# Two weight blocks of 141 granules laid apart, in wider weight tiles

## The chip, the cores and the metric

The kernel runs on one core of one Trainium2 chip. Its metric is device time in microseconds of that core, the median of several runs. Float32 is used throughout; a product of two matrices is made of three matmuls on fp32r halves (high x high, high x low, low x high).

## The reference

A block of two layers (normalisation, bidirectional mLSTM, dilated attention, gated MLP) is followed by a second block of two layers on the same 256 tokens and on 256 context tokens (attention with a window and a sink, MLP; then a gated linear scan, MLP). Cut to what matters:

```
for l in range(2):                                   # first block, x: 256 x 1024
    u = h * (1 + sc1) + sh1                          # sc, sh, g from c_act @ w_ada[l]
    z = u @ w_in[l]                                  # mLSTM q, k, v, o, gates; attention; branch gates
    y = (sig(g_a) * (mlstm(z) @ w_a) + sig(g_b) * (dilated_attention(z) @ w_b)) @ w_out
    h = layer_norm(ALPHA * h + g1 * y)
    u = h * (1 + sc2) + sh2
    h = layer_norm(ALPHA * h + g2 * ((silu(u @ w1) * (u @ w3)) @ w2))     # 1024 -> 2816 -> 1024
for i in range(2):                                   # second block, tokens and context
    x = x + m[2] * rms_norm(attention(modulate(x)) if i == 0 else gated_scan(modulate(x)))
    x = x + m[5] * rms_norm(relu(modulate(x) @ w_mlp_in) ** 2 @ w_mlp_out) # 1024 -> 4096 -> 1024
```

## The kernel before

All weights stand in one tensor in the order of their use, packed on the host into granules of 128 x 1024 numbers (512 KB). `plan()` lists them with a key each: `va`, `at`, `qk`, `o`, `br`, `wb`, `wa`, `wo` for the mixers of the first block, `w1`, `w3`, `w2` for its MLPs, `qkv`, `awo`, `mi`, `mo` for the second block's attention and MLPs, `gq`, `gg`, `gk`, `gv`, `gwo` for its scan. 591 of them go through the main stream; 192 more (`w_ada`, `w_mod_2`) are read by VectorE alone.

`gran(key, mm, post)` takes the next granule and issues its matmuls. `ahead` runs before each: it loads raw tiles up to five granules ahead (SP's queue, four tiles), makes wh, the fp32r high half, three ahead (ScalarE, four tiles) and wl, the low half, two ahead (VectorE, three tiles). The order of all work is written out by hand: generators in a list (`bg`) hand out a piece of attention, convolution, scan or normalisation at each `tick`, between granules.

Two shapes of granule matter here. In a "ws" granule (`mm_ws`) eight blocks of 128 columns are loaded one after the other as the stationary operand, and 256 columns of an activation stream past each, three times: wh with the high half, wh with the low half, wl with the high half. A "row" granule (`w2`) does the same with eight outputs. So each is 24 matmuls of 256 columns. In a "nat" granule (`mm_nat`) the weights stream, 512 columns at a time, 12 matmuls.

```
    def mm3(self, out, wh, wl, act, first, last):
        mm = self.nc.tensor.matmul
        mm(out, wh, act[:, 0], start=first, stop=False)
        mm(out, wh, act[:, 1], start=False, stop=False)
        mm(out, wl, act[:, 0], start=False, stop=last)
```

The pools lie in SBUF one behind another: constants, `wp` (raw, wh, wl and three `araw`, each 4,096 bytes a partition), a gap of 448 bytes, the ring `t4` of 25 tiles of 4,096 bytes (activations as uT, hT, yat, mT, hid, attention's kT and qT, residuals), the ring `t2` of eight tiles of 2,048 bytes, and small tiles. A new t4 tile takes the place that has been free longest and waits for its last reader.

In the profile nearly all instructions of TensorE and VectorE carry line 338, the wrapper that records them, so that tiles tell them apart: "mm<-uT,wh" is a matmul of a ws granule, "aux<-mlg,wh" one of w2, "aux<-wh,hid" one of a nat granule of the MLP, "trb<-kT,qT" attention's scores. The copies to wh are line 471, made in `ahead`.

Of the kernel before, what the change touches and what calls it, by code (L numbers as in the profile page):

```python
# [9 lines left out]
F32 = mybir.dt.float32  # L10
F32R = mybir.dt.float32r
BF16 = mybir.dt.bfloat16
AF = mybir.ActivationFunctionType
ALU = mybir.AluOpType
# [145 lines left out]
         [("wb", 2), ("wb", 3)] + [("br", j) for j in range(8)])  # L160
ADA_ORDER = (1, 0, 2, 4, 3, 5)
PLAN, NMAIN = plan()
GIDX = {e[0]: i for i, e in enumerate(PLAN)}


def pack_weights(inp):
    out = np.empty((len(PLAN), 128, 1024), np.float32)
    for i, (key, w, l, kind, r0, c0) in enumerate(PLAN):
        W = inp[w][l]
        if kind == "ws":  # L170
            out[i] = W[:, c0:c0 + 128].reshape(8, 128, 128).transpose(1, 0, 2).reshape(128, 1024)
        elif kind == "nat":
            out[i] = W[r0:r0 + 256, c0:c0 + 512].reshape(2, 128, 512).transpose(1, 0, 2).reshape(128, 1024)
        elif kind == "wsb":
            out[i] = W[r0:r0 + 512, c0:c0 + 256].reshape(4, 128, 256).transpose(1, 0, 2).reshape(128, 1024)
        elif kind == "colT":
            out[i] = W[:, c0:c0 + 128].T
        elif kind == "row":
            out[i] = W[r0:r0 + 128, c0:c0 + 1024]
        elif kind == "gates":  # L180
            t = np.zeros((128, 8, 4, 32), np.float32)
            t[:, :, :, 0:4] = W[:, c0:c0 + 16].reshape(8, 128, 4, 4).transpose(1, 0, 2, 3)
            out[i] = t.reshape(128, 1024)
        elif kind == "gdown":
            t = np.zeros((128, 8, 4, 32), np.float32)
            t[:, :, 0:2, 0:16] = W.reshape(2, 8, 128, 16).transpose(2, 1, 0, 3)
            out[i] = t.reshape(128, 1024)
    return out

# [94 lines left out]
def host(inp):  # L286
    inp = {k: np.asarray(v) for k, v in inp.items()}
    r = {"w": pack_weights(inp), "vec": pack_vecs(inp), "x": np.ascontiguousarray(inp["x"][0][ORDER]),
         "abias": attention_bias(), "mmask": mlstm_masks(), "rope": rope_tables(), "bmask": block2_masks(),
         "c": np.ascontiguousarray(np.concatenate([cols(inp[k]) for k in ("c", "c_2", "c_ctx_2")], 1)),  # L290
         "ctx": np.ascontiguousarray(inp["ctx_2"][0]),
         "ln": np.ascontiguousarray(np.broadcast_to(np.stack([inp["ln2_g"][1], inp["ln2_b"][1]])[:, None], (2, 128, 1024))),
         "wup": np.ascontiguousarray(inp["gla_w_gate_up_2"][0])}
    return r
# [14 lines left out]
class Views(list):  # L309


    def __init__(self, views, pair):
        super().__init__(views)
        self.pair = pair


class Lazy:
# [5 lines left out]
    def __getitem__(self, k):  # L323
        return self.f(k)
# [52 lines left out]
class Kernel:  # L377
# [55 lines left out]
        return self.p2.tile(list(shape), dt, tag="t2", name=name, bufs=8)  # L433

    def t4(self, name, shape, dt=F32):
        return self.p4.tile(list(shape), dt, tag="t4", name=name, bufs=25)

    def tv(self, name, shape):

# [20 lines left out]
    def ahead(self, n):  # L460

        nc = self.nc
        while True:
            if self.nload < min(self.nlo + self.RAWS, n + self.LOAD + 1, NMAIN):
                t = self.wp.tile([128, 1024], F32, tag="raw", name="raw", bufs=self.RAWS)
                nc.sync.dma_start(out=t, in_=self.i["w"][self.nload])
                self.raws[self.nload] = t
                self.nload += 1
            elif self.nhi < min(self.nload, n + self.HI + 1):
                wh = self.wp.tile([128, 1024], F32R, tag="wh", name="wh", bufs=4)  # L470
                nc.scalar.activation(out=wh, in_=self.raws[self.nhi], func=AF.Copy)  # L471
                self.hi[self.nhi] = wh
                self.nhi += 1
            elif self.nlo < min(self.nhi, n + self.LO + 1):
                raw, wh = self.raws.pop(self.nlo), self.hi.pop(self.nlo)
                wl = self.wp.tile([128, 1024], F32R, tag="wl", name="wl", bufs=3)
                nc.vector.tensor_tensor(out=wl, in0=raw, in1=wh.bitcast(F32), op=ALU.subtract)
                self.W[self.nlo] = wh, wl
                self.nlo += 1
            else:  # L480
                break

    def gran(self, key, mm, post=None):

        self.run_deferred()
        w = self.G(key)
        mm(*w)
        if post is not None:
            self.later(1, post)
        self.tick()  # L490
# [57 lines left out]
    def ada_load(self, n, tile=None):  # L548
        for it in self.adaq[:n]:
            key = it[:4]  # L550
            if key not in self.adaraw:
                t = tile() if tile else self.wp.tile([128, 1024], F32, tag="araw", name="araw", bufs=3)
                self.nc.sync.dma_start(out=t, in_=self.i["w"][GIDX[key]])
                self.adaraw[key] = t

    def ada_step(self, ahead=3):
        nc = self.nc
        self.ada_load(ahead)
        w, l, v, j, cs, bias = self.adaq.pop(0)
        g = self.adaraw.pop((w, l, v, j))  # L560
        for c, dst in cs:
            junk = g if c is cs[-1][0] else self.p.tile([128, 1024], BF16, tag="junk", name="junk", bufs=1)
            nc.vector.tensor_tensor_reduce(out=junk, in0=g, in1=c, scale=1.0, scalar=0.0, op0=ALU.mult, op1=ALU.add,
                                           accum_out=dst[:, j:j + 1])
        self.ada_left[(w, l, v)] -= 1
        if self.ada_left[(w, l, v)] == 0 and bias is not None:
            for c, dst in cs:
                nc.vector.tensor_tensor(out=dst, in0=dst, in1=bias, op=ALU.add)
# [33 lines left out]
    def first_ws(self, keys, out, act, between=None):  # L602

        w, ahead = [], (self.HI, self.LO)

        def part(n, ks):
            for k in ks:
                c = slice(k * 128, k * 128 + 128)
                self.mm3(out[:, n * 256:n * 256 + 256], w[n][0][:, c], w[n][1][:, c], act(k), n == 0 and k == 0, n == 1 and k == 7)
        for n, key in enumerate(keys):  # L610
            self.HI, self.LO = (a - n for a in ahead)
            self.gran(key, lambda wh, wl: (w.append((wh, wl)), part(n, range(6))))
        if between is not None:
            between()
        part(0, (6, 7))
        self.HI, self.LO = ahead
        self.ahead(self.cur - 1)
        part(1, (6, 7))
# [22 lines left out]
    def last_nat(self, key, act, banks, done):  # L641

        w, ahead = [], (self.HI, self.LO)
        for kp in (2, 3):
            self.HI, self.LO = (a + 2 - kp for a in ahead)
            self.gran(key(kp), lambda wh, wl: (w.append((wh, wl)), self.mm_nat(kp, act, banks, (0,))(wh, wl)))
        done(0)
        for _ in range(3):
            self.tick(False)
        for kp in (2, 3):  # L650
            self.mm_nat(kp, act, banks, (1,))(*w[kp - 2])
        done(1)
        self.HI, self.LO = ahead
# [1602 lines left out]
```

## Time and profile before

| | us |
|---|---|
| median of 3 runs (lowest, highest) | 2083.51 (2081.5, 2088.59) |
| the profiled execution, its own time | 2092.44 |
| its span, first to last instruction | 2090.7 |
| TensorE busy in it | 2030.9 |
| VectorE busy | 1586.6 |
| ScalarE busy | 1149.3 |

The profile is one execution, and its time is not the median. "Busy" of TensorE counts the modelled length of each matmul, which overlaps that of the next; what a matmul costs in a stream is the distance from its start to the next one's start. In a window over the profile, x is the number of instructions that overlap it.

### The profile page before, as it was taken

To read this page: it belongs to the slowest core of one execution; us is meant where nothing else is said; L and a number is where in the kernel's file an instruction comes from. 1 tells how busy PE (TensorE), PEld (TensorE's weight loads), DVE (VectorE), ACT (ScalarE), POOL (GpSimd) and SP (SyncE) were. 2 spreads that over 40 slices of the span, in tenths; PEclk is the share of its full clock that TensorE was granted. 3 is DMA by queue.
4 is the path that set the end of the run, shared out by engine and by line. 5 is a ranking of instruction groups with operands and counts; after the bars stand their busy time and mean duration, and the time that the engine had idled before them with its cause. 6 is when DMAs were issued, how large, how long until landed. Compare 5 with 4: busy or idle time off the path is not lost.

```text
span 2090.7 us, 38245 instructions
## 1 busy us (share of the span) xinstructions
PE 2030.9 (97%) x15176; PEld 1888.9 (90%) x15176; DVE 1586.6 (76%) x2717; ACT 1149.3 (55%) x1968; POOL 45.1 (2%) x63
## 2 busy tenths in 40 slices
PE   7999999999999999998999999999999999999998
PEld 6999998899998989998999988899998989877997
DVE  7788988799978989988899776777563485466555
ACT  5756665655546656665744455556542464445444
POOL 0000000000000000000000000000000010000000
PEclk9999999999999999999999999999999999999999
DMA  9786566598876886555589755115553352214553
GB/s 340 281 320 213 192 235 221 187 315 305 304 254 228 284 274 233 187 202 186 167 290 358 274 196 176 61 56 176 191 183 101 115 181 75 77 65 155 188 191 132
DMA packets 120884, 426.88 MB, mean 204 GB/s; under 512 B 13664, under 2 KB 18528, under 8 KB 120704
## 3 DMA queue, kind: packets, MB, share of 16 engines
q1 hardware_dynamic: 120704, 424.43, 59.1%
q8 instruction: 119, 1.95, 0.4%
q14 instruction: 61, 0.50, 0.1%
HBM read 423.33 MB, written 1.05 MB: 203 GB/s over the span
## 4 chain that ended last, share of the span: by engine, by line
PE 87%; DVE 7%; ACT 4%; issue 1%; DMA 1%; POOL 0%; DVEq 0%; POOLq 0%; SPq 0%; ACTq 0%
PE mm L338 54%; PE aux L338 28%; PE trb L338 5%; DVE wl L338 1%; ACT wh L471 1%; DVE yg L338 1%; POOL rs L674 0%; ACT xh L1467 0%; DVE mtmp L338 0%; DMA raw<-in_w 0%; DVE xh L338 0%; DVE x L338 0%; DVE araw L338 0%; ACT ah L912 0%; DVE ee L338 0%
## 5 line engine op out<-in xcount | busy, mean ns | idle before, releaser
L338 DVE TENSOR_TENSOR wl<-raw,wh 128x1024 fp32r<-128x1024 f32 x591 | 718.7, 1221 | 153.1 <-PE aux L338 71.5
L471 ACT ACTIVATE wh<-raw 128x1024 fp32r<-128x1024 f32 x591 | 623.6, 1059 | 336.2 <-PE mm L338 117.7
L338 PE MATMUL mm<-uT,wh 128*128 128x256 f32 x3488 | 622.3, 282 | 0.0
L338 PEld LDWEIGHTS mm<-uT,wh 128*128 128x128 f32 x3488 | 531.7, 188 | 2.2 <-ACT va L814 0.3
L338 PE MATMUL mm<-uT,wl 128*128 128x256 f32 x1744 | 487.0, 279 | 0.0
L338 PE MATMUL mm<-hT,wh 128*128 128x256 f32 x1888 | 339.4, 283 | 4.8 <-ACT y L1772 2.1
L338 PEld LDWEIGHTS mm<-uT,wl 128*128 128x128 f32 x1744 | 329.6, 189 | 0.0
L338 PEld LDWEIGHTS mm<-hT,wh 128*128 128x128 f32 x1888 | 292.7, 190 | 11.5 <-ACT y L1772 2.3
L338 PE MATMUL mm<-hT,wl 128*128 128x256 f32 x944 | 265.8, 282 | 0.0
L338 DVE CUSTOM_DVE_ANT_0 araw<-araw,silu 128x1024 f32<-128x1024 f32 x192 | 233.2, 1220 | 8.4 <-DMA araw<-in_w 5.9
L338 PE MATMUL aux<-wh,hid 128*128 128x512 f32 x640 | 199.9, 394 | 0.0
L338 PEld LDWEIGHTS mm<-hT,wl 128*128 128x128 f32 x944 | 181.4, 192 | 0.0
L338 PEld LDWEIGHTS aux<-wh,hid 128*128 128x128 f32 x640 | 117.7, 188 | 23.6 <-DVE hid L338 0.2
L338 DVE TENSOR_TENSOR r<-r 128x256 f32<-128x256 f32 (+1 forms) x88 | 39.5, 448 | 117.4 <-ACT r L1905 117.3
L338 PE MATMUL aux<-mlg,wh 128*128 128x256 f32 x704 | 127.1, 283 | 0.0
L338 PE MATMUL aux<-wl,hid 128*128 128x512 f32 x320 | 124.8, 390 | 0.0
L338 PEld LDWEIGHTS aux<-mlg,wh 128*128 128x128 f32 x704 | 107.3, 188 | 0.0
L1905 ACT ACTIVATE r<-mm 128x256 f32<-128x256 f32 (+1 forms) x88 | 35.7, 406 | 125.1 <-PE mm L338 125.1
L338 PE MATMUL aux<-mlg,wl 128*128 128x256 f32 x352 | 98.8, 281 | 0.0
L674 POOL TENSOR_TENSOR rs<-ve,mhalf 128x1 f32<-128x1 f32 (+1 forms) x48 | 41.8, 871 | 2040.5 <-DVE ve L338 1853.0
L338 DVE CUSTOM_DVE_ANT_0 junk<-araw,silu 128x1024 bf16<-128x1024 f32 x64 | 77.9, 1218 | 0.0
L338 PE MATMUL mm<-wh,hT 128*128 128x256 f32 (+1 forms) x352 | 76.8, 316 | 0.6 <-DVE qs L338 0.6
(365 smaller groups left out, 3081.7 us busy)
## 6 DMA issues: line engine op xcount, KB each, us to landing
raw<-in_w SPq DMA_DIRECT2D x591, 512.0 KB, 3.9
araw<-in_w SPq DMA_DIRECT2D x192, 512.0 KB, 5.2
abias<-in_abias SPq DMA_DIRECT2D x32, 192.0 KB, 5.6
xc<-in_ctx SPq DMA_DIRECT2D x4, 512.0 KB, 6.1
x<-in_x SPq DMA_DIRECT2D x2, 512.0 KB, 4.2
gb<-in_ln SPq DMA_DIRECT2D x2, 512.0 KB, 5.4
out_x<-x SPq DMA_DIRECT2D x4, 256.0 KB, 2.0
mk<-in_mmask SPq DMA_DIRECT2D x1, 512.0 KB, 5.9
```

The source lines that it names most:

```text
L338: return f(*a, **k)
L471: nc.scalar.activation(out=wh, in_=self.raws[self.nhi], func=AF.Copy)
L674: nc.gpsimd.tensor_tensor(out=rs, in0=ve, in1=self.mhalf[:, 0:n], op=ALU.pow)
L1905: nc.scalar.activation(out=r[:, 0:n], in_=ps, func=AF.Relu)
```

## The change

The tensor of weights gets rows of 1,088 numbers in place of 1,024. For 141 granules of the main stream, chosen by key in `moved`, the host puts blocks 2 to 7 first, at columns 0 to 767, and blocks 0 and 1 behind them at columns 816 to 1,071; 48 columns between are zero. The tiles raw, wh and wl are 1,088 wide; load, copy and subtraction take 1,072 columns of such a granule and 1,024 of any other. `Moved` maps a block's old columns to the new ones, so that the matmuls and their order stay as they are. The ring t4 has 24 tiles in place of 25.

```
+WIDE = 1088
+def moved(key):
+    n = key[0]
+    if n in ("w3", "w2"):
+        return key[1] == 0
+    if n == "w1":
+        return key[1] == 1 and key[2] % 2 == 0
+    if n in ("o", "br", "wa", "wo"):
+        return key[2] % 2 == 0
+    if n == "qk":
+        return key[4] == 0
+    if n == "mi":
+        return key[2] % 4 == 0
+    return n in ("gq", "gg", "gk") and key[1] % 2 == 0
+
+class Moved:
+    def __init__(self, t):
+        self.t = t
+    def __getitem__(self, i):
+        rows, c = i
+        n = 816 if c.start < 256 else -256
+        return self.t[rows, c.start + n:c.stop + n]
...
+        if i < NMAIN and moved(key):
+            t = wide[i, :, 0:1024].copy()
+            wide[i] = 0
+            wide[i, :, 0:768] = t[:, 256:]
+            wide[i, :, 816:1072] = t[:, 0:256]
...
-        return self.p4.tile(list(shape), dt, tag="t4", name=name, bufs=25)
+        return self.p4.tile(list(shape), dt, tag="t4", name=name, bufs=24)
...
-                t = self.wp.tile([128, 1024], F32, tag="raw", name="raw", bufs=self.RAWS)
-                nc.sync.dma_start(out=t, in_=self.i["w"][self.nload])
+                t = self.wp.tile([128, WIDE], F32, tag="raw", name="raw", bufs=self.RAWS)
+                c = self.width(self.nload)
+                nc.sync.dma_start(out=t[:, c], in_=self.i["w"][self.nload][:, c])
...
-                nc.scalar.activation(out=wh, in_=self.raws[self.nhi], func=AF.Copy)
+                c = self.width(self.nhi)
+                nc.scalar.activation(out=wh[:, c], in_=self.raws[self.nhi][:, c], func=AF.Copy)
...
-                nc.vector.tensor_tensor(out=wl, in0=raw, in1=wh.bitcast(F32), op=ALU.subtract)
-                self.W[self.nlo] = wh, wl
+                nc.vector.tensor_tensor(out=wl[:, c], in0=raw[:, c], in1=wh.bitcast(F32)[:, c], op=ALU.subtract)
+                self.W[self.nlo] = (Moved(wh), Moved(wl)) if moved(PLAN[self.nlo][0]) else (wh, wl)
...
+    def width(self, n):
+        return slice(0, 1072 if moved(PLAN[n][0]) else 1024)
...
-                self.nc.sync.dma_start(out=t, in_=self.i["w"][GIDX[key]])
+                self.nc.sync.dma_start(out=t, in_=self.i["w"][GIDX[key]][:, 0:1024])
```

## Rows read from the trace of the kernel before

**Rows 1.** The page, parts 1 and 4: busy time, and the chain by engine.
```profile
PE 2030.9 (97%) x15176; PEld 1888.9 (90%) x15176; DVE 1586.6 (76%) x2717; ACT 1149.3 (55%) x1968; POOL 45.1 (2%) x63
...
PE 87%; DVE 7%; ACT 4%; issue 1%; DMA 1%; POOL 0%; DVEq 0%; POOLq 0%; SPq 0%; ACTq 0%
```
**Rows 2.** Windows, TensorE: length, busy (x matmuls), granted clock, DMA share, GB/s.
```profile
606.00:626.00 20.00, 20.00 (x179) 1.00 0.55 185
...
1042.00:1218.00 176.00, 176.00 (x1496) 1.00 0.82 295
...
1498.00:1518.00 20.00, 20.00 (x172) 1.00 0.54 178
...
1609.00:1652.00 43.00, 43.00 (x368) 1.00 0.27 91
285.00:294.00 9.00, 9.00 (x79) 1.00 0.54 173
```
**Rows 3.** Timeline, TensorE, at 608 us: start, length, line, operation, count.
```profile
607.84 0.39 PE L338 MATMUL aux<-mlg,wh 128*128 128x256 f32 x2
...
608.52 0.39 PE L338 MATMUL aux<-mlg,wh 128*128 128x256 f32 x2
```
**Rows 4.** Timeline, TensorE, at 1100 us.
```profile
1099.89 0.40 PE L338 MATMUL mm<-uT,wh 128*128 128x256 f32 x2
...
1100.60 0.40 PE L338 MATMUL mm<-uT,wh 128*128 128x256 f32 x2
```
**Rows 5.** Timeline, TensorE, at 575 us: w1, scores, w3.
```profile
574.44 0.39 PE L338 MATMUL mm<-uT,wh 128*128 128x256 f32 x2
...
575.12 0.64 PE L338 MATMUL trb<-kT,qT 128*128 128x256 f32 x4
575.60 0.40 PE L338 MATMUL mm<-uT,wh 128*128 128x256 f32 x2
...
576.30 0.28 PE L338 MATMUL mm<-uT,wh 128*128 128x256 f32 x1
```
**Rows 6.** Timeline, TensorE, at 421 us: transposes, scores, w3.
```profile
420.81 0.49 PE L338 MATMUL trb<-ident,qs 128*128 128x128 f32 x3
421.06 0.73 PE L338 MATMUL trb<-kT,qT 128*128 128x256 f32 x4
421.62 0.41 PE L338 MATMUL mm<-uT,wh 128*128 128x256 f32 x2
...
421.98 0.39 PE L338 MATMUL mm<-uT,wh 128*128 128x256 f32 x2
...
422.32 0.39 PE L338 MATMUL mm<-uT,wh 128*128 128x256 f32 x2
```
**Rows 7.** Timeline, TensorE: starts of four mi granules of the last loop.
```profile
1918.08 0.40 PE L338 MATMUL mm<-hT,wh 128*128 128x256 f32 x2
...
1923.58 0.40 PE L338 MATMUL mm<-hT,wh 128*128 128x256 f32 x2
...
1941.13 0.40 PE L338 MATMUL mm<-hT,wh 128*128 128x256 f32 x2
...
1946.73 0.40 PE L338 MATMUL mm<-hT,wh 128*128 128x256 f32 x2
```
**Rows 8.** The page, part 5: the copies to wl and wh.
```profile
L338 DVE TENSOR_TENSOR wl<-raw,wh 128x1024 fp32r<-128x1024 f32 x591 | 718.7, 1221 | 153.1 <-PE aux L338 71.5
L471 ACT ACTIVATE wh<-raw 128x1024 fp32r<-128x1024 f32 x591 | 623.6, 1059 | 336.2 <-PE mm L338 117.7
```
**Rows 9.** Waits, whole span: us in total, times, longest.
```profile
ACT wh L471 <- DMA raw<-in_w: 28.2, 17, 4.0
...
PEld mm L338 <- DVE wl L338: 7.1, 7, 2.6
```
**Rows 10.** The page, part 6: KB of a load, median us from issue to landing.
```profile
raw<-in_w SPq DMA_DIRECT2D x591, 512.0 KB, 3.9
```
**Rows 11.** Timeline: TensorE at 1300 us, ScalarE at 1303.6 us.
```profile
1300.02 0.39 PE L338 MATMUL aux<-wl,hT 128*128 128x512 f32 x1
...
1303.63 0.60 ACT L1659 ACTIVATE qT<-trb 128x512 fp32r<-128x512 f32 x1 [0.94 <-PE trb L338]
```

More of the change, by code (lines that the diff above doesn't have):

```diff
@@ L162 @@
 PLAN, NMAIN = plan()
+WIDE = 1088
 GIDX = {e[0]: i for i, e in enumerate(PLAN)}
+def moved(key):
[18 more added lines that the diff above has]
+        return self.t[rows, c.start + n:c.stop + n]
 def pack_weights(inp):
-    out = np.empty((len(PLAN), 128, 1024), np.float32)
+    wide = np.zeros((len(PLAN), 128, WIDE), np.float32)
+    out = wide[:, :, 0:1024]
     for i, (key, w, l, kind, r0, c0) in enumerate(PLAN):
@@ L187, in pack_weights @@
             out[i] = t.reshape(128, 1024)
-    return out
+        if i < NMAIN and moved(key):
[3 more added lines that the diff above has]
+            wide[i, :, 816:1072] = t[:, 0:256]
+    return wide
 VOFF = {}
@@ L469, in ahead @@
             elif self.nhi < min(self.nload, n + self.HI + 1):
-                wh = self.wp.tile([128, 1024], F32R, tag="wh", name="wh", bufs=4)
-                nc.scalar.activation(out=wh, in_=self.raws[self.nhi], func=AF.Copy)
+                wh = self.wp.tile([128, WIDE], F32R, tag="wh", name="wh", bufs=4)
+                c = self.width(self.nhi)
+                nc.scalar.activation(out=wh[:, c], in_=self.raws[self.nhi][:, c], func=AF.Copy)
                 self.hi[self.nhi] = wh
@@ L475, in ahead @@
                 raw, wh = self.raws.pop(self.nlo), self.hi.pop(self.nlo)
-                wl = self.wp.tile([128, 1024], F32R, tag="wl", name="wl", bufs=3)
-                nc.vector.tensor_tensor(out=wl, in0=raw, in1=wh.bitcast(F32), op=ALU.subtract)
-                self.W[self.nlo] = wh, wl
+                wl = self.wp.tile([128, WIDE], F32R, tag="wl", name="wl", bufs=3)
+                c = self.width(self.nlo)
+                nc.vector.tensor_tensor(out=wl[:, c], in0=raw[:, c], in1=wh.bitcast(F32)[:, c], op=ALU.subtract)
+                self.W[self.nlo] = (Moved(wh), Moved(wl)) if moved(PLAN[self.nlo][0]) else (wh, wl)
                 self.nlo += 1
```

## The prediction

> **What bounds the kernel now.** The page first: TensorE is busy 97% of the span and owns 87% of the chain that ended last, VectorE 7% [rows 1]. So the time is a sum of matmul steps, and the question is what one step costs. A granule of the kind that the change touches (eight blocks of 128 columns, three matmuls of 256 columns on each, 24 in all) is read in two views. Windows that hold nothing else give the step, start to start: 20 us with 179 matmuls at 606 us, less the two or three that only reach in, are 113.3 ns a matmul; 176 us with 1,496 at 1042 us are 117.8; those at 1498, 1609 and 285 us are of the long sort too [rows 2]. The granted clock is 1.00 in all of them (the 2.4 GHz level) and TensorE has no idle time in them, so no other engine makes the difference. The timeline shows it inside a granule: two triples take 0.68 us at 607.8 and 0.71 at 1099.9 [rows 3, 4]. Identical instructions thus have two steps, 4.5 ns apart, and a stream keeps the one it has for granule after granule, some 60 of them at 1042 us: a lock with a memory, chosen anew where something breaks the stream.
>
> **What changes the lock.** By the allocation of the kernel before, every weights block lies 64 bytes (modulo 256) off the operand that streams past it: wh starts at byte 37,760 of a partition, the ring t4 at 79,168, and blocks and operands are multiples of 512 bytes apart. The attention products kT x qT have both operands in the ring, a distance of 0. They make a free experiment in the loop of layer 0's MLP: at 574.4 us w1 runs at 0.68 us for two triples; four kT x qT matmuls follow without a gap in 0.48 us, 120 ns each; behind them w3 takes 0.70 for two triples and stays long [rows 5]. There are sixteen such passages from 421 to 576 us, and fifteen come out long like this last one. The first, at 421.06, comes out of transposes and so at another phase: w3's first triple takes 0.36 us, the next 0.34, and short it stays [rows 6]. So a few matmuls at distance 0 cost 120 ns each and do change the lock; which way seems to hang on the phase in which they end.
>
> **The change part by part.**
>
> *The moved blocks.* By the rule of `moved`, 141 granules of the plan get blocks 0 and 1, their first six matmuls, 816 columns behind the tile's start: 3,264 bytes, 192 modulo 256. With the 64 from before that is distance 0. These 846 matmuls then cost 120 by the nearest row [rows 5]: +2.2 ns where the step is long today, +6.7 where it is short. Bounds: 113.3 (distance 0 does nothing here) to 121 (the longest triple of a lock in change [rows 6]), so -3.8 to +6.5 us for all.
>
> *What follows them.* The other 18 matmuls, and the granules behind up to the next break, start from a new phase. No row shows a passage from a long step through distance 0, which is what most of these granules would be. Bounds: all come out short, or all long. I take short, for two reasons: long is the state that most of them are in, so that a changed phase mostly gains; and the one passage entered otherwise than the fifteen came out short [rows 6]. Then, with 4.5 ns a step:
> - MLP of layer 1, 1042 to 1218 us [rows 2]: 1,494 long steps, kicked every six granules: -6.7, and 66 steps at +6.7 ns: -6.3 us.
> - MLP of layer 0: w3 and w2, each moved, long in all but some five of 22 rounds: 33 granules at 18 x 4.5 - 6 x 2.2 = 68 ns, less 11 short ones that lose 40: -1.8 us.
> - mi of the block behind, eight granules a time: four stretches like that at 1498 and one of 43 us at 1609 [rows 2], together 119 us or 1,010 long steps: -4.5, plus ten kicks of 40 ns: -4.1 us.
> - The last loop alternates mi with mo. A pair takes 5.50 us at 1918 and 5.60 at 1941 [rows 7]; the slower form holds to the end: 25 pairs of 0.1, less seven kicks: -2.2 us.
> - The heads (213 to 318, 846 to 946 us): 285 to 294 is long [rows 2]; if three fifths of the 205 us are, 1,040 steps, and three quarters of them are reached before a break: -3.5, less 40 kicks of about 25 ns: -2.5 us.
> - wa, wo and the gated scan's granules, 26 that are mostly short: +1.0 us.
>
> *The copies.* 48 more columns on wh and wl: 1,221 ns for 1,024 columns gives +57 ns on VectorE, 1,059 gives +50 on ScalarE [rows 8]; 141 times that is 8.1 and 7.1 us, hidden behind 2.7 us of matmuls a granule. Without that cover: weight loads waited for wl seven times, 7.1 us in all [rows 9], so 7 x 57 ns = 0.4 us. Taken as 0.
>
> *The loads.* Rows of 4,288 bytes at a pitch of 4,352: about 0.2 us on a landing of 3.9 [rows 10], in the same order on SP's queue. ScalarE waited for raw 17 times [rows 9]; all of them 0.2 later is the upper bound, 3.4 us; taken as 0, since loads run up to five granules ahead.
>
> *Wider tiles, ring of 24.* Eleven tiles grow by 256 bytes, the ring moves by 11 x 256, so the distance modulo 256 of all that isn't moved stays 64. Every second weights tile now differs by 256 bytes, which no row shows; bounds are the steps seen, 113.3 to 120; taken as today's. The ring, replayed with 24 tiles (a new tile takes the one free longest): the closest reuse is ScalarE's qT at 1303.63 over an hT whose last matmul began at 1300.02 and took 0.39 [rows 11]. With 3.2 us of room there is no new wait; behind a late qT the copies of wh would queue, three granules ahead of their use.
>
> Sum: -6.3 - 1.8 - 4.1 - 2.2 - 2.5 + 1.0 = -15.9 us on the profiled execution's 2092.4 (span 2090.7 and 1.7 around it): 2076.5. That execution lies 8.9 above the runs' median of 2083.5; in the same ratio the median becomes 2067.7, say 2068.
>
> The Trainium skill speaks against all of this: "TensorE: Matmul & The Clock Gate", section "Step-by-step: what each phase is for", gives TensorE two independent SBUF read ports and says that loading the next weights takes no read bandwidth from the running matmul. By that the place of a block couldn't matter, and the sum would be 0. The trace disagrees in so far as identical matmuls take 113.3, 117.8 and 120 ns; that it is reads that collide, it doesn't show.
>
> **The rivals.**
>
> *Distance 0 always leaves the long step* (slower). For it: fifteen passages of sixteen [rows 5]. Against: they were all entered from the short step, and were four matmuls, not six. It decides as soon as the phase after six is that after four. The 846 cost 2.2 or 6.7 ns (2.5 us), and some 1,350 short ones (an estimate: 18 in each of 50 granules, half as many behind them) turn long, 6.0: +8.5, 2101 in the profile, 2092 as a median. Chance 0.16.
>
> *The lock is untouched.* The six cost their own and the old state returns, or the place of a block is no cause at all. +2.5 us or nothing: 2084 to 2086. For it: the lock outlasts granule borders, where the operands jump too. Against: the passage at 575 us [rows 5]. Chance 0.14.
>
> *A toss at each kick.* The phase differs from place to place and half come out short: the mean of -15.9 and +8.5, -4: 2080. For it: the two outcomes in [rows 5, 6]. Chance 0.14.
>
> **How the numbers follow.** The forecast, short behind the kicks, has 0.56, and by itself 2060 to 2074 (kicks at 113.3 and the heads reached whole, or a third of the stretches not reached). The range reaches over the toss and the untouched lock into the slower case: 2060 to 2090, which leaves out about 2 in 10. What a measurement of this kernel can tell from no change is about 0.3%, 6 us. Faster: 0.56 and a third of the toss, 0.61. Within: most of the untouched lock and the rest of the toss, 0.21. Slower: the first rival and a little of the untouched, 0.18.
>
> **What would show it.** Right: the layer-1 MLP's windows near 113.3 ns from its first w1 on; six steps near 120 at the head of a moved granule; w3 and w2 of layer 0 short; the last loop's pairs at 5.50. Wrong at the exit: 117.8 in all these, and in wa and wo too. Wrong in what was taken as 0: other steps in granules that weren't moved, tile by tile; ScalarE waiting before a tile of t4; weight loads waiting for wl more often than seven times.

## The result, and the profile after

The changed kernel is slower: 2101.45 us median (2099.7 to 2106.19, four runs) against 2086.05 beside it, ratio 1.0069 (95% interval 1.0045 to 1.0092). Timed once more in five rounds it gave 1.0082 (1.0064 to 1.0100). The forecast was 2068. The profiled execution took 2101.86 us, its span 2100.1, which is 9.4 above the span of the one before.

The page of the changed kernel, parts 1 and 4, against [rows 1]:
```profile
PE 2039.1 (97%) x15176; PEld 1895.8 (90%) x15176; DVE 1594.1 (76%) x2717; ACT 1154.4 (55%) x1968; POOL 44.4 (2%) x63
...
PE 87%; DVE 7%; ACT 4%; issue 1%; DMA 1%; POOL 1%; POOLq 0%; DVEq 0%; SPq 0%; ACTq 0%
```
Nothing new has become the bound; TensorE's own time has grown. Its windows in the changed kernel, placed some 10 us later than those of [rows 2] because the same work comes later (columns as there):
```profile
1052.00:1228.00 176.00, 176.00 (x1496) 1.00 0.86 303
1509.00:1529.00 20.00, 20.00 (x172) 1.00 0.60 186
1620.00:1663.00 43.00, 43.00 (x367) 1.00 0.29 89
```
The MLP of layer 1, where 6.3 us were to be won, has the same 1,496 matmuls in 176 us as before. And the stretch that was short in [rows 2], 179 matmuls in 20 us, is now long:
```profile
613.00:633.00 20.00, 20.00 (x172) 1.00 0.53 168
```
The timeline of the changed kernel shows where it turns, at the head of a moved w3:
```profile
611.20 0.39 PE L373 MATMUL mm<-uT,wh 128*128 128x256 f32 x2
...
611.54 0.40 PE L373 MATMUL mm<-uT,wh 128*128 128x256 f32 x2
...
611.90 0.40 PE L373 MATMUL mm<-uT,wh 128*128 128x256 f32 x2
...
612.25 0.40 PE L373 MATMUL mm<-uT,wh 128*128 128x256 f32 x2
...
612.61 0.40 PE L373 MATMUL mm<-uT,wh 128*128 128x256 f32 x2
```
Each row starts a triple (the wl matmul is left out). The last short triple takes 0.34 us; the first of the moved blocks takes 0.36, that is 120 ns a matmul; then 0.35 and 0.36 and so on: long, 117.8 in the mean.

The second loss stands in the list of waits of the changed kernel (engine, what waited, for what: us, times, longest), against [rows 9]:
```profile
PEld mm L373 <- DVE wl L373: 8.5, 6, 6.3
...
PE mm L373 <- DVE wl L373: 6.1, 1, 6.1
```
Weight loads wait for wl six times, not more often than before, but one wait is 6 us long, in wo. The timelines of VectorE and TensorE at that place; first the kernel before:
```profile
349.10 1.22 DVE L338 CUSTOM_DVE_ANT_0 araw<-araw,silu 128x1024 f32<-128x1024 f32 x1
...
350.25 1.22 DVE L338 CUSTOM_DVE_ANT_0 araw<-araw,silu 128x1024 f32<-128x1024 f32 x1
...
352.10 2.35 DVE L338 TENSOR_TENSOR wl<-raw,wh 128x1024 fp32r<-128x1024 f32 x2
...
353.37 0.40 PE L338 MATMUL mm<-mT,wl 128*128 128x256 f32 x1 [2.40 <-DVE wl L338]
```
then the changed one:
```profile
350.54 1.22 DVE L373 CUSTOM_DVE_ANT_0 araw<-araw,silu 128x1024 f32<-128x1024 f32 x1
...
351.68 1.22 DVE L373 CUSTOM_DVE_ANT_0 araw<-araw,silu 128x1024 f32<-128x1024 f32 x1
...
352.83 1.22 DVE L373 CUSTOM_DVE_ANT_0 araw<-araw,silu 128x1024 f32<-128x1024 f32 x1
...
355.30 1.22 DVE L373 CUSTOM_DVE_ANT_0 araw<-araw,silu 128x1024 f32<-128x1024 f32 x1 [1.24 <-DMA araw<-in_w]
...
357.15 2.40 DVE L373 TENSOR_TENSOR wl<-raw,wh 128x1072 fp32r<-128x1072 f32 x2
358.47 0.29 PEld L373 LDWEIGHTS mm<-mT,wl 128*128 128x128 f32 x1 [6.31 <-DVE wl L373]
358.47 0.58 PE L373 MATMUL mm<-mT,wl 128*128 128x256 f32 x1 [6.10 <-DVE wl L373]
```
VectorE makes four rows of the modulation (`araw`) ahead of the wl that TensorE needs, and not two; the fourth waits for its load. The order of VectorE's instructions is thus another. The reason is in code that the diff doesn't touch. While the program is built, a class `Core` books a cost for each TensorE and VectorE instruction, and `tick` adds a modulation row only while VectorE, by these costs, isn't late:

```
self.dve = max(self.dve, self.pe - self.SLACK) + 90 + math.prod(x.shape[1:]) / 0.96
...
if self.adaq and not self.hold and self.nc.late < self.room:
    self.ada_step()
```
A wl of 1,072 columns is booked 50 ns (48 / 0.96) longer. So rows are put off, and what is still missing where the next normalisation's factors are needed is made there at once (`ada_need`), ahead of the wl. The orders of TensorE and ScalarE are the same in both kernels; those of VectorE and of SP's loads differ.

The wait has a tail. Behind it the granted clock of TensorE is down, as the window of the changed kernel shows. In the kernel before the shorter wait ends at 353.37 us, and in this execution the clock behind it stays up; its window comes second:
```profile
358.00:363.00 5.00, 4.53 (x23) 0.57 0.83 275
```
```profile
352.00:358.00 6.00, 4.63 (x40) 1.00 0.95 321
```
By the starts in the trace 16 matmuls behind the wait take 213 ns (the 1.2 GHz level) in place of 113. In the repeated run of the changed kernel they are 21, and the row is at 0.50:
```profile
358.00:363.00 5.00, 4.79 (x22) 0.50 0.88 293
```

### The profile page after: what moved, and what is told of

It reads as the page before. It is cut to its first block, busy times and chain, and to the rows that moved or that the text cites. A ratio compares the mean times of both kernels' runs of the same rounds, so it can differ in the third digit from the quotient of the medians.

```text
span 2100.1 us, 38254 instructions
## 1 busy us (share of the span) xinstructions
PE 2039.1 (97%) x15176; PEld 1895.8 (90%) x15176; DVE 1594.1 (76%) x2717; ACT 1154.4 (55%) x1968; POOL 44.4 (2%) x63
## 4 chain that ended last, share of the span: by engine, by line
PE 87%; DVE 7%; ACT 4%; issue 1%; DMA 1%; POOL 1%; POOLq 0%; DVEq 0%; SPq 0%; ACTq 0%
PE mm L373 54%; PE aux L373 28%; PE trb L373 5%; DVE wl L373 1%; ACT wh L508 1%; POOL rs L715 1%; DVE yg L373 1%; DMA raw<-in_w 0%; DVE x L373 0%; DVE xh L373 0%; DVE mtmp L373 0%; ACT u L944 0%; ACT xh L1508 0%; ACT ah L953 0%; DVE ee L373 0%
## 5 line engine op out<-in xcount | busy, mean ns | idle before, releaser
L373 DVE TENSOR_TENSOR wl<-raw,wh 128x1024 fp32r<-128x1024 f32 (+1 forms) x591 | 725.8, 1232 | 154.7 <-PE aux L373 70.8
L508 ACT ACTIVATE wh<-raw 128x1024 fp32r<-128x1024 f32 (+1 forms) x591 | 629.0, 1069 | 349.4 <-PE mm L373 117.3
L373 DVE CUSTOM_DVE_ANT_0 araw<-araw,silu 128x1024 f32<-128x1024 f32 x192 | 233.1, 1220 | 9.1 <-DMA araw<-in_w 6.9
```

What stands on the lines that cost most here:

```text
L373: return f(*a, **k)
L508: nc.scalar.activation(out=wh[:, c], in_=self.raws[self.nhi][:, c], func=AF.Copy)
```

## The experiments

| run | median us | ratio to before (95%) |
|---|---|---|
| e1, distance 0 with before's order | 2099.11 | 1.0075 (1.0056 to 1.0095) |
| e2, order alone | 2091.89 | 1.0029 (1.0012 to 1.0045) |
| e3, distance 64 in the changed kernel | 2092.32 | 1.0041 (1.0027 to 1.0055) |
| e4, wide tiles and ring of 24 alone | 2085.43 | 1.0011 (0.9994 to 1.0027) |
| e5, gap of 32 (distance 192) | 2072.08 | 0.9943 (0.9925 to 0.9961) |
| e6, one block at distance 0 | 2096.07 | 1.0058 (1.0037 to 1.0080) |
| e7, all at 128 | 2117.63 | 1.0163 (1.0137 to 1.0189) |
| e8, all at 0 | 2118.77 | 1.0169 (1.0146 to 1.0192) |
| e9, all at 192 | 2108.54 | 1.0105 (1.0081 to 1.0129) |
| e10, gap of 16 (distance 128) | 2071.17 | 0.9936 (0.9912 to 0.9960) |
| e11, gap of 32 in 348 granules | 2075.39 | 0.9948 (0.9925 to 0.9970) |
| e12, one granule at 192 | 2084.55 | 1.0000 (0.9984 to 1.0015) |
| e13, two granules at 0 | 2088.49 | one run |
| e14, the changed kernel again | 2103.50 | 1.0082 (1.0064 to 1.0100) |
| e15, e1 again, beside e14 | 2097.94 | 1.0054 (1.0034 to 1.0075) |

**e1, e15: the changed kernel in the order of before.**
```diff
+        n = math.prod(x.shape[1:])
+        n = 1024 if n == 1072 else n
-        ... + 90 + math.prod(x.shape[1:]) / 0.96
+        ... + 90 + n / 0.96
```


> The changed kernel, but the pacing model that decides where VectorE does its modulation rows books every copy to wl as 1,024 columns, so that the order of all engines' instructions is that of the kernel before; blocks, distances, copies and loads stay as changed. Theory 1 (two causes: the order costs one longer wait before wo, the distance costs pace): TensorE's wait for wl at about 350 us is 2.4 us again and not 6.1, the time falls by 3 to 4 us from the changed kernel's, ratio to before about 1.005, six steps near 119.5 ns at the head of a moved granule and 117 behind them as in the changed kernel. Theory 2 (pace alone): the ratio stays at 1.007. Theory 3 (the order alone): the ratio is 1.000 to 1.001.

> The changed kernel with the order of before once more, beside the changed one: 3 to 4 us below it if order and distance add up, level with it if the wait is taken back; in both cases ratio to before 1.005 to 1.0075.

The wait is 2.5 us at its longest again, and the clock behind it stays up in both. Waits and window of e15, where the wait ends at 353.84 us:
```profile
PE mm L373 <- DVE wl L373: 4.4, 2, 2.5
```
```profile
352.00:358.00 6.00, 4.16 (x36) 1.00 0.90 329
```
By the first pair alone (1.0069 and 1.0075) the order would be worth nothing. Timed side by side, e15 is 5.6 us below e14. Theory 3, the order alone, falls: with the order of before 1.0054 to 1.0075 are left.

> The changed kernel once more, beside the one with before's order. If order and distance add up, it is 3 to 4 us (0.0017) slower than the one with before's order, ratio to before about 1.008 to 1.009; if the order's wait is taken back further on, both have the same ratio, 1.007.

**e2: the order alone.**
```diff
                 nc.vector.tensor_tensor(out=wl, in0=raw, in1=wh.bitcast(F32), op=ALU.subtract)
+                if moved(PLAN[self.nlo][0]):
+                    nc.dve += 48 / 0.96
```


> The kernel before, with the order of the changed one: the pacing model books 48 more columns for the copies to wl of the 141 granules, and nothing else is changed. Theory 1: the wait for wl at about 350 us is 6.1 us in place of 2.4, ratio 1.002 (3.7 of 2086 us). Theory 2 (pace alone): 1.000. Theory 3 (the order alone): 1.006 to 1.007.

Waits of e2, and the window behind the wait:
```profile
PE mm L354 <- DVE wl L354: 6.2, 2, 6.0
```
```profile
356.10:361.10 5.00, 5.00 (x27) 0.59 0.91 332
```
The wait comes with the order, without any moved block. I had expected its 3.7 us; with the low clock it is 3.6 of wait and 17 matmuls at 100 ns more, 5.3, and the interval (2.5 to 9.4 us) holds both. The low clock is not the order's alone. In the profiled executions it follows the wait in all four with the order of the changed kernel (the changed kernel, e2, e3, e14), but also in five of the thirteen with the order of before and its shorter wait (e4, e6, e9, e12, e13). The window of e4, against those of the kernel before and e15 above:
```profile
352.00:358.00 6.00, 5.29 (x32) 0.72 0.95 331
```
So the longer wait is shown to be the order's; the 1.7 us behind it are in part a matter of the execution.

**e3: distance 64 in the changed kernel.**
```diff
-            wide[i, :, 816:1072] = t[:, 0:256]
+            wide[i, :, 832:1088] = t[:, 0:256]
-        n = 816 if c.start < 256 else -256
+        n = 832 if c.start < 256 else -256
```
with width 1,088, booked as 1,072.

> The changed kernel with a gap of 64 columns in place of 48: the two blocks stand 832 columns behind the tile's start, a multiple of 256 bytes, so that their distance to the streamed operand is 64 bytes (modulo 256) like that of all others. Order as in the changed kernel, copies and loads 16 columns longer still. Theory 1: the six steps are 113 or 118 ns like the rest, moved granules have before's mix, the wait of 6.1 us stays: ratio 1.002. Theory 2 (pace alone): 1.000. Theory 4 (the copies, loads or wider tiles cost it): 1.007 or more.

Here the steps at the moved blocks are 116.3 in the mean, against 116.4 at the same places of e4, where nothing is moved. So moving alone does nothing, and theory 1 holds. The ratio of 1.0041 isn't told apart from the 1.0029 of the order alone, so nothing of it can be put down to copies, loads and tiles.

**e4: wide tiles and the ring of 24, nothing moved.**
```diff
 def moved(key):
+    return False
```


> The changed kernel with no granule moved: weights tiles of 1,088 columns, rows of 1,088 in the tensor, the ring of 24, copies and loads of 1,024 columns, the order of before. Theories 1 to 3: ratio 1.000, since 320 and 64 bytes (modulo 512) gave the same mix of steps in the changed kernel. Theory 4 (wider tiles or the smaller ring): 1.003 to 1.007.

No cost that the interval tells from none. The trace of e4 shows something else. The same order at the same distances gives another step in some stretches. A window of the kernel before, and the same of e4:
```profile
1618.00:1648.00 30.00, 30.00 (x257) 1.00 0.29 103
```
```profile
1618.00:1648.00 30.00, 30.00 (x267) 1.00 0.32 102
```
In the profiled execution before this stretch was long, in e2, e3 and e4 it is short. Its span was 2090.7, that of e4 2084.3. Part of what I counted as 117.8 was a draw of that execution.

**e5, e10: other gaps, order of before.**
```diff
-            wide[i, :, 816:1072] = t[:, 0:256]
+            wide[i, :, 800:1056] = t[:, 0:256]     # e10: 784:1040
-        n = 816 if c.start < 256 else -256
+        n = 800 if c.start < 256 else -256         # e10: 784
```


> The changed kernel with a gap of 32 columns in place of 48 (the two blocks 3,200 bytes behind the tile's start, distance 192 bytes modulo 256 from the streamed operand in place of 0), order of the kernel before. Theory 1 (only distance 0 has the step of 119 to 120 ns and leaves the long step): the six steps are 113 or 118, the granules behind them have the mix of the run at distance 64, ratio 1.000 to 1.003, and the gated-scan, wa and wo stretches are short again. Rival (any jump of distance throws the stream into the long step): steps behind the blocks 117 to 118 everywhere, ratio 1.006 or more.

> The changed kernel with a gap of 16 columns (the two blocks 3,136 bytes behind the tile's start, distance 128 bytes modulo 256), order of the kernel before. Theory 1c (192 alone leads to the short step): the six steps are 118 to 119 ns, as when all lie at 128, and the MLP of layer 1 is at 117.8 behind them: ratio 1.003 to 1.007. Rival (any distance but 0 leads to the short step): 113.3 in the MLP of layer 1, ratio 0.995 to 0.998.

For e5 every expectation missed on the same side, for e10 the rival holds: both kernels are faster than before, by 0.6%. The MLP of layer 1 in a window of e5, and in one of e10:
```profile
1050.00:1200.00 150.00, 150.00 (x1326) 1.00 0.88 316
```
```profile
1050.00:1200.00 150.00, 150.00 (x1324) 1.00 0.88 315
```
That is 113.3 ns a matmul (150 us over 1,324, two reach in), where the kernel before and the changed one have 1,275. This is the gain that I forecast, at another distance. A moved w1 in e10's timeline:
```profile
1042.90 0.39 PE L373 MATMUL mm<-uT,wh 128*128 128x256 f32 x2
...
1043.25 0.40 PE L373 MATMUL mm<-uT,wh 128*128 128x256 f32 x2
...
1043.61 0.39 PE L373 MATMUL mm<-uT,wh 128*128 128x256 f32 x2
...
1043.95 0.39 PE L373 MATMUL mm<-uT,wh 128*128 128x256 f32 x2
```
The two triples of the moved blocks take 0.35 and 0.36, the next 0.34: the stream pays some 30 ns and is short again.

Counted over the moved granules that an unbroken stream of granules of 24 leads into (the six steps ahead and the first eight under 130 ns, no kT x qT among the six; by the median of the six ahead and of the steps from the ninth on):

| distance of the two blocks | from long | from short |
|---|---|---|
| 0 (changed kernel) | 39: 39 long | 12: 11 long |
| 64 (e3) | 25: 25 long | 26: 26 short |
| 128 (e10) | 8: 8 short | 41: 41 short |
| 192 (e5) | 6: 6 short | 44: 44 short |

Fifteen more granules, w3 of layer 0, stand right behind kT x qT: long in the changed kernel, short in e5 and e10, each time all of them. Where a step of over 130 ns (a wait, or a matmul of 512 columns) breaks the stream the outcome is mixed: in the changed kernel 20 of the other 75 moved granules come out short.

**e6: three matmuls at distance 0.** Blocks 1 to 7 first, block 0 at column 944.
```diff
-            wide[i, :, 816:1072] = t[:, 0:256]
+            wide[i, :, 944:1072] = t[:, 0:128]
```


> The changed kernel with only block 0 set apart (three matmuls at distance 0 in place of six; blocks 1 to 7 first, block 0 at column 944, again 192 bytes modulo 256), order of the kernel before. Theory 1a (distance 0 leaves the long step whatever the number): the second of the moved blocks returns to 117.8, the rest as in the run with two blocks, ratio about 1.006. Theory 1b (the number of matmuls decides the phase they end in): the MLP of layer 1, 1042 to 1218 us, comes out at 113.3 ns, some 6 us or more below the run with two blocks, ratio 1.002 or less.

The MLP of layer 1 stays long, 1,276 matmuls in 150 us, and all 64 moved granules that no step of over 130 ns breaks come out long, 14 of them from the short step. There theory 1a holds: in an unbroken stream three, four or six matmuls at distance 0 lead to the long step. Behind a break it doesn't. Seventeen w2 of layer 0 follow small products or transposes of the mixers, with a first step of some 200 ns. They come out long behind six matmuls at 0 and short behind three, all seventeen each time (in e1, which has the order of e6, six lead to long as well). One of them (starts of triples, behind the moved blocks) in the changed kernel, then in e6:
```profile
474.38 0.40 PE L373 MATMUL aux<-mlg,wh 128*128 128x256 f32 x2
...
474.73 0.40 PE L373 MATMUL aux<-mlg,wh 128*128 128x256 f32 x2
```
```profile
468.11 0.39 PE L373 MATMUL aux<-mlg,wh 128*128 128x256 f32 x2
...
468.45 0.39 PE L373 MATMUL aux<-mlg,wh 128*128 128x256 f32 x2
```
A triple takes 0.35 us in the first and 0.34 in the second. So behind this break the number decides, as theory 1b has it.

**e7, e8, e9: every weights block at another distance.**
```diff
-        nc.gpsimd.memset(self.p4.tile([128, 112], F32, name="gap"), 0.0)
+        nc.gpsimd.memset(self.p4.tile([128, 96], F32, name="gap"), 0.0)   # e8: 128, e9: 80
```


> The kernel before with one number changed: the spacer ahead of the activations' ring has 96 columns in place of 112, so that the ring stands 64 bytes lower and every weights block lies 128 bytes (modulo 256) from the operand that streams past it, in place of 64. Theory 1 (only distance 0 is dear): the same two steps of 113.3 and 117.8 ns, ratio 0.995 to 1.005 by where the stream falls. Rival (each distance has its own pace): another step in all stretches, whose sign isn't known.

> The kernel before with a spacer of 128 columns in place of 112: the ring stands 64 bytes higher and every weights block lies at distance 0 (modulo 256) from the operand that streams past it. Theory 1: every step in a stream is 119 to 120 ns in place of 116.3 in the mean, 10,080 matmuls by 3 to 4 ns, 30 to 40 us: ratio 1.015 to 1.02. Rival (the six dear steps are the passage from one distance to another, not distance 0 itself): steps of 113 and 118, ratio 1.000 to 1.005.

> The kernel before with a spacer of 80 columns in place of 112: the ring stands 128 bytes lower, every weights block of a granule of 24 lies 192 bytes (modulo 256) from the operand that streams past it, and in the granules of 512-column matmuls, where weights and operand change places, the distance is 64 in place of 192. Theory 1c (192 has the short step and leads back to it): nearly all of the 10,080 steps are 113.3 in place of 116.3 in the mean, the granules of 512 columns are dearer by less than 4 ns a matmul: 15 to 28 us less, ratio 0.987 to 0.993. Rival (both steps exist at 192 as they do at 64, and it is the passage that leads to the short one): stretches at 117.8 remain, ratio 0.995 to 1.005.

The MLP of layer 1 in windows of e7, e8 and e9:
```profile
1050.00:1200.00 150.00, 150.00 (x1266) 1.00 0.87 314
```
```profile
1050.00:1200.00 150.00, 150.00 (x1253) 1.00 0.87 314
```
```profile
1050.00:1200.00 150.00, 150.00 (x1276) 1.00 0.88 317
```
At 128 a step takes 118.7 ns, at 0 119.9. At 192 both steps exist, and the stream is in the long one nearly everywhere (117.45 in the mean of all). So my theory 1c, that 192 has the short step, is wrong, and its rival holds: it is the passage to 192 and back that leaves the short step. The rival's ratio (up to 1.005) was missed all the same, at 1.0105. In e9 the matmuls of 512 columns, now at 64, take 233.1 in place of 229.8. Theory 1 for e7 is wrong too: 128 is nearly as dear as 0. For e8 it holds.

The Trainium skill, "TensorE: Matmul & The Clock Gate", section "Step-by-step: what each phase is for", has two independent SBUF read ports, so that a load of weights takes nothing from the running matmul. By that rule one number in a spacer shouldn't cost 22 to 35 us, as it does here by the ratios of e9 and e8, and the measurement decides. That it is the two reads that collide, no run shows.

**e11: the gap of 32 in 348 granules.** `moved` returns true for all granules of its twelve kinds.

> The kernel with the gap of 32 columns, with the two blocks moved in all 348 granules of the twelve kinds in place of 141. Theory 1c: long steps remain only in the granules of attention's matrices and in the first six steps behind a break; the last loop's granules and the first block's heads come down to 113.3 to 114; about 3 to 6 us less than with 141, ratio 0.991 to 0.993. Rival (more copies of 1,056 columns take back what is won): 0.994 or more.

No gain over e5 (2075.39 and 2072.08, intervals overlap). Neither expectation is told from the other by the interval (0.9925 to 0.9970). The granules that e5 doesn't move average 114.2 ns a step, 114.3 in e5: more passages found little left to turn.

**e12, e13: one passage.**
```diff
 def moved(key):
+    return key[0:3] == ("w1", 1, 0)                        # e12, gap of 32
+    return key[0:3] in (("w3", 0, 19), ("w1", 1, 0))       # e13, gap of 48
```


> Wider tiles and the ring of 24, with one granule moved in the whole kernel: the first w1 of layer 1 (at some 1,034 us), its two blocks at the gap of 32 columns (distance 192), order of the kernel before. Theory 1d (a passage from distance 64 over 192 and back leads to the short step, and the step is then kept): the MLP of layer 1, 1042 to 1218 us in the kernel before, runs at 113.3 ns to its end, 1,496 steps by 4.5 ns, 6.7 us less in this stretch; all others as in the run with wide tiles alone; ratio 0.996 to 0.998. Rival (the short step has to be renewed: each granule's change of tiles can lose it): 113.3 only for some granules, then 117.8; ratio 0.999 to 1.001.

> Wider tiles and the ring of 24, with two granules of the kernel moved at the gap of 48 columns (distance 0), order of the kernel before: the w3 of layer 0 at some 604 us, where the stream is short before it and short to 628, and the first w1 of layer 1 at some 1,034, where it is long. Theory 1 (out of distance 0 the stream comes long from either step): from the first on the steps are 117.8 to 628 us, and the MLP of layer 1 stays at 117.8. The forecast's rule (the phase changes, long becomes short): the MLP of layer 1 at 113.3, some 6.7 us less; the stretch at 606 us long. Rival (the state of the stream is no matter of distance 0 alone): both as before, 113.3 and 117.8.

The MLP of layer 1 in e12, six matmuls moved in the whole kernel:
```profile
1050.00:1200.00 150.00, 150.00 (x1326) 1.00 0.89 319
```
The layer 0 stretch and the MLP of layer 1 in e13:
```profile
609.00:629.00 20.00, 20.00 (x172) 1.00 0.58 185
...
1050.00:1200.00 150.00, 150.00 (x1276) 1.00 0.88 312
```
In e4, which differs only in that nothing is moved, the first of these holds 179:
```profile
609.00:629.00 20.00, 20.00 (x179) 1.00 0.61 194
```
One passage over 192 turns the MLP of layer 1 short to its end, 1,578 of its 1,584 steps; one over distance 0 turns a short stretch long and leaves a long one long. The profiled span of e12 is 5.2 us below e4's, but its median is not told apart from it (1.0000 and 1.0011, each within some 0.0016): why the 6.7 us of that stretch don't show there stays open.

## Why the prediction was wrong

**The step that failed** is in "What follows them": "I take short, for two reasons". Out of distance 0 an unbroken stream comes long, 39 times in 39 from the long step, 11 in 12 from the short one, and alone in e13. The row that was against it stood there: fifteen of sixteen passages in [rows 5]. I set them aside as entered from the other step, and let the one exception [rows 6] decide. The rival "Distance 0 always leaves the long step" was the right one.

Setting them aside was a wrong reading too. "No row shows a passage from a long step through distance 0", I wrote, and of the fifteen that "they were all entered from the short step". Three were entered from the long one, at 482.25, 523.59 and 564.92 us of the kernel before, and came out long. The first of them, w1, scores, w3:
```profile
481.55 0.40 PE L338 MATMUL mm<-uT,wh 128*128 128x256 f32 x2
...
482.25 0.64 PE L338 MATMUL trb<-kT,qT 128*128 128x256 f32 x4
482.73 0.40 PE L338 MATMUL mm<-uT,wh 128*128 128x256 f32 x2
...
483.44 0.40 PE L338 MATMUL mm<-uT,wh 128*128 128x256 f32 x2
```
Two triples take 0.70 us ahead of the scores and 0.71 behind them. So the trace before held the very passage that most moved granules would make. The one exception came behind a break (its first matmul takes 202 ns), and behind a break the outcome is another matter, as e6 shows. That much of my idea of a phase stays possible; for the unbroken stream it was wrong.

Its terms: the MLP of layer 1, -6.3 forecast, gave nothing (1,496 matmuls in 176 us before and after). Layer 0's MLP, -1.8, became +1.7 (sum of the starts' distances over its w1, w3 and w2). The heads, -2.5, became about +2.3 (qk 1.5, o 0.5, br 0.3). wa alone lost 2.5, but only 1.2 of it in pace: 15 of its matmuls ran at 213 ns behind a wait at some 961 us, where the execution before kept its clock. Of the mi stretches of the second block (-4.1) I counted as long what in e4 was short: stalls apart, all mi of that MLP gave 0.1 against the execution before and lost 3.3 against e4's.

The last loop has the time that was forecast, but not by the forecast's way; that is luck. Most pairs of mi and mo take 5.49 us in the changed kernel, against 5.59, and e4 has 5.59 too. But a pair that begins with a moved mi takes 5.64. One such pair and the mi behind it, in the changed kernel:
```profile
1957.72 0.40 PE L373 MATMUL mm<-hT,wh 128*128 128x256 f32 x2
...
1960.56 0.63 PE L373 MATMUL aux<-wh,hid 128*128 128x512 f32 x2
...
1963.36 0.41 PE L373 MATMUL mm<-hT,wh 128*128 128x256 f32 x2
...
1966.10 0.62 PE L373 MATMUL aux<-wh,hid 128*128 128x512 f32 x2
```
The moved mi is long (2.84 us for its 24), as elsewhere. The twelve 512-column matmuls of mo behind it take 233 ns each. The short step (2.74 us for 24) begins with the next mi, which isn't moved.

**A term that was missing**: the order. I read the 48 columns as engine time only, and wrote that the loads come in the same order on SP's queue; they don't. VectorE's copies are 46 ns dearer by the page (1,232 against 1,221 in the mean of 591, of which 141 grew; 57 forecast), ScalarE's 42 (50 forecast), and both lie behind the matmuls as said. But the copy's length also enters the pacing model, and moved two modulation rows to wo: 3.7 us of wait in the profiled execution, 5.2 with the low clock behind it.

**What was right**: a matmul at distance 0 takes 119.3 ns (651 steps of the changed kernel with both blocks there; 120 forecast). Wider tiles and the smaller ring cost nothing that e4 shows, longer copies and loads nothing that e3 tells apart; weights tiles that differ by 256 bytes have the same mix of steps (116.2 and 116.5 ns in the granules not moved).

**The size of the rival.** I worked out +8.5 us. Four of the 141 granules serve two streams with their blocks, so that 870 matmuls are at distance 0 and not 846. Here is the changed kernel against e4 and before, by starts in the trace, positions in which either stalls (above 130 ns, 245 for 512 columns) apart:

| part | matmuls | e4 | before | changed | us against e4 |
|---|---|---|---|---|---|
| those at distance 0 | 790 | 116.4 | 116.5 | 119.1 | +2.1 |
| the others of moved granules | 2,528 | 115.9 | 116.2 | 117.4 | +3.7 |
| granules not moved | 6,479 | 115.9 | 116.5 | 116.35 | +3.0 |
| 512 columns | 2,136 | 229.9 | 229.8 | 230.7 | +1.6 |

In all 10.4 us; the ratios of e15 and e1 to the kernel before come to 11 and 16, that of e4 to 2. The first three parts, 8.8, are near the 8.5. But the granules that weren't moved lost 3.0 for the 2.0 that I had, since they were short in more places than in the execution I read; and the 512-column matmuls take the state over too, which I left out. (The 384 matmuls of 256 columns in nat granules, 0.7 us shorter, are not in the table.) Against the profiled execution before, the order's 5.2 us and the first three parts' 3.9 make nearly the 9.4 of the span; the rest (+1.9 in 512 columns, +1.5 at the start, where the clock rises later, -2.9 in other stalls and small work) nearly cancels.

**Open**: what makes 0 lead to one step and 128 and 192 to the other wasn't found; the trace shows starts, not reads. So is why behind a break six and three matmuls at 0 lead to different steps. The order's cost, 5.6 us by e14 and e15 and 5.2 by the trace, lies within the interval of e2 in both cases; how much of it is the low clock varies from one execution to the next.

## What to carry to other kernels

When one instruction stands in two persistent steps, the passage between two relative positions of its operands sets the step: try several passages on one granule and read a window behind it, before laying out the whole stream by a guess of the sign. If one outcome in sixteen speaks for the forecast, the fifteen are the forecast; and before a row is set aside for its state, read the steps ahead of each one. Where a program orders its work by booked costs, ask of every changed size what it is booked at, and compare the orders of the instructions before any time is worked out.

## What the runs showed of the hardware

- Matmuls of 256 fp32r columns, start to start at a granted clock of 1.00, by the distance modulo 256 of weights and streamed operand when all lie there: 119.9 ns at 0, 118.7 at 128, 113.3 or 117.8 at 64 and at 192. With 512 columns (steps under 245): 228.2 at 0 (e8), 233.1 at 64 (e9), 232.4 at 128 (e7), 229.8 at 192 (before), in the mean.
- Between unbroken streams at 64, six matmuls at 128 (e10) or 192 (e5) lead to the short step; six at 0 (changed kernel), four (before) or three (e6) to the long one. The step then lasts, for 1,578 matmuls in e12.
- A wait of TensorE of 6.0 to 6.1 us was followed by 13 to 21 matmuls at 213 ns in four of four profiled executions, granted clock 0.50 to 0.68 over the 5 us behind it. Behind the wait of 2.4 to 2.5 us at the same place the clock stayed at 1.00 in eight of thirteen (the kernel before and e15 among them); in e4, e6, e9, e12 and e13 it was 0.66, with 13 to 15 matmuls at 213 ns.
